# Packet sizes in a DMA-bound rotation: five of twelve slabs loaded with 8 KB and stored with 16 KB packets, the other seven the other way round, and no one-row store first

## The chip, the cores, the metric

One core of one Trainium2 chip; the other cores are idle. The metric is device time in microseconds (us) of one execution, as the median over executions; a profiled execution beside it leaves a trace.

## The reference

```python
x = np.random.randn(32, 3, 256, 256).astype(np.float32)
np.rot90(x, k=-1, axes=(-2, -1)).astype(np.float32)
```

96 images of 256 x 256 float32 are turned by a quarter. Nothing is computed: 25.17 MB come in and 25.17 MB go out.

## The kernel before

The 96 images are cut into 12 slabs of 8 images, 2.10 MB each (called "2 MB" below, and half of it "1 MB"). A slab lies in a tile of 128 partitions x 2 x 2048 float32. What decides the size of a DMA packet is how much of one partition is contiguous in device memory: 8 rows of 1 KB (the `(n i p r)` views, 128 partitions) give 8 KB packets; 16 rows (the `(n i m r)` view, 64 partitions for one half) give 16 KB packets. Half `i` of a 16 KB slab lies in every second partition, `units[n][i::2]`.

```python
    RI, RO = 16, 8
    ...
    plain = (0, last - 2, last - 1, last)
    ...
    ld8_v  = rows_in.rearrange("(n i p r) w -> n p i (r w)", i=I, p=P, r=RO)
    ld16_v = rows_in.rearrange("(n i m r) w -> n i m (r w)", i=I, m=Q * K, r=RI)
    st_v   = rows_out.rearrange("(n i p c) w -> n p i (c w)", i=I, p=P, c=RO)
    ...
    for n in range(n_slabs):              # all loads are issued first, on the sync queue
        for i in range(I):
            if n in plain:
                nc.sync.dma_start(out=units[n][:, i], in_=ld8_v[n][:, i])
            else:
                nc.sync.dma_start(out=units[n][i::I].rearrange("p i f -> p (i f)"), in_=ld16_v[n, i])

    for n in range(n_slabs):              # slab n is turned into the tile of slab n - 1
        t_in, t_out = units[n], units[n - 1] if n else turned0    # slab 0 into PSUM
        ...                               # two VectorE transposes of 128 x 2048 for each slab
        if n == 1:
            nc.sync.dma_start(out=st_v[n][:, 0, :W], in_=t_out[:, 0, :W])      # the one-row store
            nc.sync.dma_start(out=st_v[n][:, 0, W:], in_=t_out[:, 0, W:])
            nc.sync.dma_start(out=st_v[n][:, 1], in_=t_out[:, 1])
        elif n in (2, 3):
            for i in range(I):
                nc.sync.dma_start(out=st_v[n][:, i], in_=t_out[:, i])
        elif n:
            nc.sync.dma_start(out=st_v[n], in_=t_out)

    for i in range(I):                    # slab 0 last: PSUM -> SBUF by ScalarE, then stored
        nc.scalar.copy(out=units[last][:, i], in_=turned0[:, i])
    nc.sync.dma_start(out=st_v[0], in_=units[last])
```

So before, slabs 0, 9, 10 and 11 are loaded and stored in 8 KB packets, slabs 1 to 8 loaded in 16 KB and stored in 8 KB. The first store goes out as one row (1 KB) of each partition, then the other seven.

## Time and profile before

| | before |
|---|---|
| time | 123.53 us (123.49 to 123.58, 3 runs) |
| span of the profiled execution | 121.8 us |
| 16 DMA engines busy | 98.1% of the span |
| VectorE busy | 92.7 us (76%), 24 transposes |
| packets | 5888, of which 640 are semaphore writes |

How to read it: the page cuts the span into 40 slices; the DMA row has the busy share of 16 DMA engines in tenths, the GB/s row what they moved. The prediction below shows these rows.

One more reading of the trace is used throughout the document. For every packet the trace has a start, a duration and a size. Spreading each packet's bytes evenly over its duration and adding up the engines gives the bytes moved up to each moment; the time between two successive multiples of 2.10 MB is the time that the queue needed for one slab.

### The profile page before, as it was taken

To read this page: it belongs to the slowest core of one execution; us is meant where nothing else is said; L and a number is where in the kernel's file an instruction comes from. 1 tells how busy PE (TensorE), PEld (TensorE's weight loads), DVE (VectorE), ACT (ScalarE), POOL (GpSimd) and SP (SyncE) were. 2 spreads that over 40 slices of the span, in tenths; PEclk is the share of its full clock that TensorE was granted. 3 is DMA by queue.
4 is the path that set the end of the run, shared out by engine and by line. 5 is a ranking of instruction groups with operands and counts; after the bars stand their busy time and mean duration, and the time that the engine had idled before them with its cause. 6 is when DMAs were issued, how large, how long until landed. Compare 5 with 4: busy or idle time off the path is not lost.

```text
span 121.8 us, 140 instructions
## 1 busy us (share of the span) xinstructions
DVE 92.7 (76%) x24; ACT 5.0 (4%) x3; POOL 0.2 (0%) x4
## 2 busy tenths in 40 slices
DVE  0199999999999999999999999999999930000000
ACT  0000000000000000000300000000000660000000
POOL 0000000000000000000000000000000000000000
DMA  3999999999999999999999999999999999999995
GB/s 86 425 436 430 430 430 430 430 430 430 430 430 430 430 430 403 430 422 420 420 397 429 430 425 425 430 425 430 428 430 430 428 430 430 425 425 428 425 430 218
DMA packets 5888, 50.33 MB, mean 413 GB/s; under 512 B 640, under 2 KB 768, under 8 KB 896
## 3 DMA queue, kind: packets, MB, share of 16 engines
q1 hardware_dynamic: 5888, 50.33, 98.1%
HBM read 25.17 MB, written 25.17 MB: 413 GB/s over the span
## 4 chain that ended last, share of the span: by engine, by line
DVE 41%; issue 33%; DMA 4%; DVEq 3%; ACT 2%
DVE u L80 31%; DVE turned L74 6%; DMA u<-in_x_dram 4%; DVE u L74 4%; DVEq L120 3%; ACT u L93 2%
## 5 line engine op out<-in xcount | busy, mean ns | idle before, releaser
L80 DVE STREAM_TRANSPOSE u<-u 128x2048 f32<-128x2048 f32 x16 | 62.4, 3945 | 0.3
L74 DVE STREAM_TRANSPOSE u<-u 128x2048 f32<-128x2048 f32 x6 | 22.8, 3931 | 0.0
L74 DVE STREAM_TRANSPOSE turned<-u 128x2048 f32<-128x2048 f32 x2 | 7.6, 3828 | 5.6 <-DMA u<-in_x_dram 5.6
L93 ACT COPY u<-turned 128x2048 f32<-128x2048 f32 x2 | 3.7, 1865 | 35.8 <-DVE u L74 35.8
L93 ACT ACT_TABLE_LOAD x1 | 1.3, 1283 | 59.7 <-DMA u<-in_x_dram 59.7
L109 POOL MEMSET const-bfloat16-1.0<- 128x1 bf16 x1 | 0.1, 101 | 0.0
L109 POOL MEMSET const-uint8-127<- 128x1 uint8 x1 | 0.1, 101 | 0.0
L109 POOL MEMSET const-float32-0.0<- 128x1 f32 x1 | 0.1, 98 | 0.2 <-issue 0.2
L109 POOL MEMSET const-float32-1.0<- 128x1 f32 x1 | 0.1, 98 | 0.0
## 6 DMA issues: line engine op xcount, KB each, us to landing
u<-in_x_dram SPq DMA_DIRECT2D x24, 1024.0 KB, 19.6
out_dram<-u SPq DMA_DIRECT2D x9, 2048.0 KB, 22.8
out_dram<-u SPq DMA_DIRECT2D x5, 1024.0 KB, 17.4
out_dram<-u SPq DMA_DIRECT2D x1, 896.0 KB, 17.5
out_dram<-u SPq DMA_DIRECT2D x1, 128.0 KB, 18.0
```

The costliest lines, as they stand in the source:

```text
L74: nc.vector.transpose(out=dst[:, :, ::-1, ::-1], in_=src)
L80: nc.vector.transpose(out=dst[:, cs], in_=src[:, cs])
L93: nc.scalar.copy(out=units[last][:, i], in_=turned0[:, i])
L109: nc = _bacc.Bacc("TRN2", target_bir_lowering=False, num_devices=1)
L120: with _tile.TileContext(nc) as tc:
```

## The change

Each quarter turn has a row side and a column side, and by choice of the layout in SBUF one of the two can have 16 KB packets. The intent: give every slab one 16 KB side (four had none), choose which side per slab, and drop the one-row store. Slabs 0, 1, 2, 10 and 11 are now loaded in 8 KB and stored in 16 KB packets, slabs 3 to 9 loaded in 16 KB and stored in 8 KB.

```diff
-    plain = (0, last - 2, last - 1, last)
+    long_st = (0, 1, 2, last - 1, last)
 ...
     for n in range(n_slabs):
+        if n in (1, 2, last - 1):
+            ld = nc.sync.dma_start(out=units[n], in_=ld_short[n])
+            continue
         for i in range(I):
-            if n in plain:
-                nc.sync.dma_start(out=units[n][:, i], in_=ld8_v[n][:, i])
+            if n in long_st:
+                ld = nc.sync.dma_start(out=units[n][:, i], in_=ld_short[n][:, i])
             else:
-                nc.sync.dma_start(out=units[n][i::I].rearrange("p i f -> p (i f)"), in_=ld16_v[n, i])
+                ld = nc.sync.dma_start(out=units[n][i::I].rearrange("p i f -> p (i f)"), in_=ld_long[n, i])
+
+    def store(n, t, i):
+        if n in long_st:
+            return nc.sync.dma_start(out=st_long[n, i], in_=t[i::I].rearrange("p i f -> p (i f)"))
+        return nc.sync.dma_start(out=st_short[n][:, i], in_=t[:, i])
 ...
-        if n in plain:
-            for i in range(I):
-                src = t_in[:, i].rearrange("p (r g c) -> p c r g", r=RO, c=RO)
-                dst = t_out[:, i].rearrange("p (c g r) -> p c r g", c=RO, r=RO)
-                nc.vector.transpose(out=dst[:, :, ::-1, ::-1], in_=src)
+        if n in long_st:
+            src = t_in.rearrange("p i (r g c) -> p c r g i", r=RS, c=RL)
+            dst = t_out.rearrange("p i f -> p (i f)").rearrange("p (c k r) -> p c r k", c=RL, r=RS)[:, :, ::-1, ::-1]
+            pieces = 2
+            for h in range(pieces):
+                cs = slice(h * RL // pieces, (h + 1) * RL // pieces)
+                nc.vector.transpose(out=dst[:, cs], in_=src[:, cs])
 ...  (the 16 KB load form keeps its transposes)
-        if n == 1:
-            nc.sync.dma_start(out=st_v[n][:, 0, :W], in_=t_out[:, 0, :W])
-            nc.sync.dma_start(out=st_v[n][:, 0, W:], in_=t_out[:, 0, W:])
-            nc.sync.dma_start(out=st_v[n][:, 1], in_=t_out[:, 1])
-        elif n in (2, 3):
+        if n in range(5, last - 1):
+            nc.sync.dma_start(out=st_short[n], in_=t_out)
+        elif n:
             for i in range(I):
-                nc.sync.dma_start(out=st_v[n][:, i], in_=t_out[:, i])
-        elif n:
-            nc.sync.dma_start(out=st_v[n], in_=t_out)
+                store(n, t_out, i)
 ...
-    nc.sync.dma_start(out=st_v[0], in_=units[last])
+    for i in range(I):
+        store(0, units[last], i)
```

More of the change, by code (lines that the diff above doesn't have):

```diff
@@ L40, with short, long @@
     P = nc.NUM_PARTITIONS
-    RI, RO = 16, 8
-    K = H // RI
+    RL, RS = 16, 8
     I = 2
-    Q = P // (K * I)
+    Q = P * RS // H
     n_slabs = B * C // (Q * I)
     last = n_slabs - 1
-    plain = (0, last - 2, last - 1, last)
-    F = RO * W
+    F = RS * W
+    long_st = (0, 1, 2, last - 1, last)
     rows_in = x.rearrange("b c h w -> (b c h) w")
     rows_out = out.rearrange("b c h w -> (b c h) w")
-    ld8_v = rows_in.rearrange("(n i p r) w -> n p i (r w)", i=I, p=P, r=RO)
-    ld16_v = rows_in.rearrange("(n i m r) w -> n i m (r w)", i=I, m=Q * K, r=RI)
-    st_v = rows_out.rearrange("(n i p c) w -> n p i (c w)", i=I, p=P, c=RO)
+    def short(rows):
+        return rows.rearrange("(n i p r) w -> n p i (r w)", i=I, p=P, r=RS)
+    def long(rows):
+        return rows.rearrange("(n i m r) w -> n i m (r w)", i=I, m=P // I, r=RL)
+    ld_short, ld_long, st_short, st_long = short(rows_in), long(rows_in), short(rows_out), long(rows_out)
     pools = [ctx.enter_context(tc.tile_pool(name=f"unit{u}", bufs=1)) for u in range(n_slabs)]
@@ L68 @@
+    def store(n, t, i):
+        if n in long_st:
+            return nc.sync.dma_start(out=st_long[n, i], in_=t[i::I].rearrange("p i f -> p (i f)"))
+        return nc.sync.dma_start(out=st_short[n][:, i], in_=t[:, i])
     for n in range(n_slabs):
         t_in, t_out = units[n], units[n - 1] if n else turned0
-        if n in plain:
-            for i in range(I):
-                src = t_in[:, i].rearrange("p (r g c) -> p c r g", r=RO, c=RO)
-                dst = t_out[:, i].rearrange("p (c g r) -> p c r g", c=RO, r=RO)
-                nc.vector.transpose(out=dst[:, :, ::-1, ::-1], in_=src)
-        else:
-            src = t_in.rearrange("p i f -> p (i f)").rearrange("p (r g c) -> p c r g", r=RI, c=RO)
-            dst = t_out.rearrange("p i (c k r) -> p c r k i", c=RO, r=RI)[:, :, ::-1, ::-1, :]
-            for h in range(2):
-                cs = slice(h * RO // 2, (h + 1) * RO // 2)
-                nc.vector.transpose(out=dst[:, cs], in_=src[:, cs])
@@ L82 @@
-        if n == 1:
-            nc.sync.dma_start(out=st_v[n][:, 0, :W], in_=t_out[:, 0, :W])
-            nc.sync.dma_start(out=st_v[n][:, 0, W:], in_=t_out[:, 0, W:])
-            nc.sync.dma_start(out=st_v[n][:, 1], in_=t_out[:, 1])
-        elif n in (2, 3):
-            for i in range(I):
-                nc.sync.dma_start(out=st_v[n][:, i], in_=t_out[:, i])
-        elif n:
-            nc.sync.dma_start(out=st_v[n], in_=t_out)
+        if n in long_st:
[5 more added lines that the diff above has]
+                nc.vector.transpose(out=dst[:, cs], in_=src[:, cs])
+        else:
+            src = t_in.rearrange("p i f -> p (i f)").rearrange("p (r g c) -> p c r g", r=RL, c=RS)
+            dst = t_out.rearrange("p i (c k r) -> p c r k i", c=RS, r=RL)[:, :, ::-1, ::-1, :]
+            for h in range(2):
+                cs = slice(h * RS // 2, (h + 1) * RS // 2)
+                nc.vector.transpose(out=dst[:, cs], in_=src[:, cs])
```

## The prediction

> **What bounds the kernel now.** I read the utilisation slices first, then the DMA queue's total, the groups of instructions, stretches of the span, packet counts of two clean stretches, and last the issue order. The slices and the queue come first because a rotation computes nothing: it moves 25.17 MB in, 25.17 MB out.
>
> ```profile
> DVE  0199999999999999999999999999999930000000
> DMA  3999999999999999999999999999999999999995
> GB/s 86 425 436 430 430 430 430 430 430 430 430 430 430 430 430 403 430 422 420 420 397 429 430 425 425 430 425 430 428 430 430 428 430 430 425 425 428 425 430 218
> q1 hardware_dynamic: 5888, 50.33, 98.1%
> ```
>
> The 16 DMA engines are full from the second slice to the last but one. VectorE, which does all transposes, is also dense but ends seven slices earlier. So the transfers set the end. 50.33 MB at 428 GB/s is 117.6 us of the 121.8 us span; the remaining 4.2 us are the start until the first bytes move (first slice, 86 GB/s), a few dips, and the end (last slice, 218 GB/s).
>
> The page's chain of waits names VectorE for 41% of the span. I do not follow it: it passes through program order, its last steps being the transposes at 90.9 us and a ScalarE copy at 98.63 us, and leaves the last 20 us of store traffic unexplained. The groups show what VectorE costs:
>
> ```profile
> L80 DVE STREAM_TRANSPOSE u<-u 128x2048 f32<-128x2048 f32 x16 | 62.4, 3945 | 0.3
> L74 DVE STREAM_TRANSPOSE u<-u 128x2048 f32<-128x2048 f32 x6 | 22.8, 3931 | 0.0
> L74 DVE STREAM_TRANSPOSE turned<-u 128x2048 f32<-128x2048 f32 x2 | 7.6, 3828 | 5.6 <-DMA u<-in_x_dram 5.6
> L93 ACT COPY u<-turned 128x2048 f32<-128x2048 f32 x2 | 3.7, 1865 | 35.8 <-DVE u L74 35.8
> ```
>
> The two forms of transpose, line 80 (16 KB load, 8 KB store) and line 74 (8 KB both ways), cost the same within 0.4%. The only wait is 5.6 us for the first load. The timeline ends with
>
> ```profile
> 98.63 1.86 ACT L93 COPY u<-turned 128x2048 f32<-128x2048 f32 x1 [1.91 <-DVE u L74]
> 100.52 0.37 SPq L94 DMA_DIRECT2D out_dram<-u  x1
> ```
>
> The last store is issued at 100.52 us and its semaphore arrives at about 121.0 us: 20.5 us, of which 4.9 us are its own 2 MB. It waits 15.6 us behind other stores. That is the slack on the compute side.
>
> Now the rate by stretch (last column), and then the packets of two stretches, 10 to 45 us (only 16 KB loads) and 75 to 115 us (only 8 KB stores):
>
> ```profile
> 10.00:45.00 35.00, 34.83 (x10) 0.00 (x0) 0.00 (x0) 1.00 1.01 430
> 47.00:60.00 13.00, 12.97 (x4) 0.28 (x1) 0.00 (x0) 1.00 1.02 423
> 60.00:64.00 4.00, 3.97 (x2) 1.00 (x1) 0.00 (x0) 1.00 1.00 396
> 75.00:115.00 40.00, 23.56 (x7) 3.73 (x2) 0.00 (x0) 1.00 1.01 428
> ```
> ```profile
> DMA packets 1147, 15.04 MB, mean 430 GB/s; under 512 B 229, under 2 KB 229, under 8 KB 229
> ```
> ```profile
> DMA packets 2217, 17.11 MB, mean 428 GB/s; under 512 B 128, under 2 KB 128, under 8 KB 128
> ```
>
> The small packets are semaphore writes. The trace's packet records give 309 ns for 8 KB, 611 for 16 KB and 9 for a semaphore write, each overlapping the next by 3 to 4 ns; so an 8 KB packet takes 305.7 ns of an engine, a 16 KB one 607.5, a semaphore 5.7. Check from the fences: (35 us x 16 - 229 x 0.0057) / 918 = 608.6 ns, and (40 x 16 - 128 x 0.0057) / 2089 = 306.0 ns. So joining two 8 KB packets saves 4 ns of 611: 0.65%. That is all the gain the packet size can give. The 8 KB loads late in the program (47 to 60 us) run at 423, about 1.6% below 16 KB loads; the 396 at 60 to 64 us is the turn from loads to stores with the one-row store in it.
>
> **What the Trainium skill says.** "DMA: Bandwidth & Descriptors", section "Where 436 GB/s comes from", puts the ceiling at 435.2 GB/s. The trace agrees (428 to 430). An estimate from that page: 50.33 MB / 435.2 = 115.7 us, so even perfect transfers would gain about 1.9 us against the 117.6 above: less than 2%. The same page, "Why small descriptors are slow (HBM only)", states a fixed overhead of about 3 cycles per packet; with that page's 850 MHz, 3.5 ns as an estimate, close to the 4 ns above. Its "Why a DMA increments its semaphore by 16 and not by 1" says the engine count is the largest number up to 16 that divides the slowest dimension, so 64 rows still use 16 engines; the 16 KB loads (64 partitions each) confirm it with 430 GB/s. "SBUF — State Buffer", section "Door 1: The DMA port swizzle", warns that partitions 0 to 63 reach only half of the ports. The 64 partitions here are every second one of 128, which reach all ports; the loads show no loss, but no store in this form has run yet.
>
> **The change, part by part.** Per engine, from the durations above; 1 MB is 8 packets of 8 KB or 4 of 16 KB. A 2 MB slab of 8 KB stores in one DMA: 16 x 305.7 + 5.7 = 4897 ns. As 16 KB stores in two DMAs: 2 x (4 x 607.5 + 5.7) = 4871 ns.
> - Stores of slabs 0, 10, 11: -26 ns each, -78.
> - Store of slab 2 (two DMAs before, 4903): -32.
> - Store of slab 1: before 8 x 42.4 (1 KB) + 8 x 268.3 (7 KB) + 8 x 305.7 + 3 x 5.7 = 4948; after 4871: -77.
> - Store of slab 4: split into two DMAs, +6. Slab 3 unchanged, 5 to 9 unchanged.
> - Loads of slabs 1 and 2: 16 KB becomes 8 KB, one DMA each: about +16 each, +32.
> - Load of slab 9: 8 KB becomes 16 KB in the stretch where 8 KB loads run at 423 and not 430: 2.10 MB / 423 - 2.10 MB / 430 = -80. Load of slab 10 in one DMA: -6.
> Sum: -78 - 32 - 77 + 6 + 32 - 80 - 6 = -235 ns, on the path, since the engines are never idle.
>
> VectorE: still 24 transposes of 128x2048, at 3.83 to 3.95 us by the rows above, so about 92.7 us. But a slab's first transpose now needs both 1 MB halves of its load, where a plain slab's needed one. VectorE starts 2.45 us later (1 MB / 428 GB/s): at 8.05 us instead of 5.6, and ends at about 101.0 instead of 98.6. Both ScalarE copies now wait for the last transpose (before, the first ran at 94.9, during it): 101.0 + 2 x 1.87 = 104.8 us with hand-over. The queue reaches slab 11's store at 121.0 - 2 x 4.9 = 111.2 and slab 0's at 116.1. Slack stays 10.2 and 11.3 us; none of it shows in the time. Issues on the sync queue stay 40 (24 + 16 before, 21 + 19 after).
>
> **The rivals.**
> 1. The turn to stores costs more without the small first store. The 396 GB/s stretch lost 4 x (1 - 396/428) = 0.30 us; a few load packets there took 470 to 580 instead of 309 ns. If the one-row store was softening this, 16 KB first packets could double the loss: -0.235 + 0.3 = +0.07 us, 123.6. If it was itself the trouble, the loss could halve: 123.15. The profile cannot tell which.
> 2. Stores from every second partition read SBUF worse than loads write it. Against: the same pattern as a load is at full rate. If it halved the rate, five slabs would take 4.9 us more each: +24 us, about 148. I give this 2 to 3%.
> 3. VectorE becomes the bound. The new transpose form (8 KB load, 16 KB store) covers 10 of 24 instructions; it must take 10.2 / 10 = 1.0 us more each before the stores run dry. The two known forms differ by 14 ns. Every further 0.1 us on each would add 1 us to the end; about 1%.
> 4. The whole effect is larger, because 16 KB stores gain more than the record of 16 KB loads says. Loads at 430 already carry excess of 1 to 3 ns; stores had none. At the ceiling of 435.2 the five slabs gain 10.49 MB x (1/428 - 1/435.2) = 0.41 us: 123.0.
>
> **Range and chances.** 123.53 - 0.235 = 123.3 us. Rivals 1 and 4 span 123.0 to 123.6, so 122.95 to 123.7 should hold 8 times in 10. Faster by over 2% needs 2.5 us, more than the distance to the ceiling: 1%. Slower by over 2% is rivals 2 and 3: 3%. The rest, 96%, is within 2%.
>
> **What would show it.** Right: the same 9s in the DMA row to the last slice; 5248 packets in all (before 5888 less 640 semaphore writes = 5248 data packets; 512 fewer by joining, 128 fewer without the cut rows: 4608; again 40 issues x 16 = 640 semaphore writes); 429 to 430 GB/s where slabs 10, 11 and 0 are stored; VectorE starting near 8 us and ending near 101; last issue near 105; span near 121.5. Wrong: gaps or a lower rate in the store slices of slabs 1, 2, 10, 11, 0 (rival 2), a new transpose row well over 3.95 us (rival 3), or a deeper dip than 397 at the turn (rival 1).

## The result, and the profile after

| | before | after |
|---|---|---|
| median, first set of rounds | 123.60 us (6 runs) | 123.44 us (6 runs) |
| median, second set of rounds | 123.82 us (11 runs) | 123.58 us (6 runs) |
| ratio after / before, first set | | 0.9981 (95%: 0.9964 to 0.9998) |
| ratio after / before, second set | | 0.9984 (95%: 0.9968 to 0.9999) |

A ratio is the mean time of one kernel's fast runs over that of the other's of the same rounds, so not quite the ratio of the medians. The change gains about 0.2 us, 0.16 to 0.19%; the two sets agree, and both 95% intervals just exclude no change.

The slices, the packet counts and the queue's total of the changed kernel:

```profile
DVE  0039999999999999999999999999999993000000
DMA  3999999999999999999999999999999999999994
GB/s 83 425 425 431 428 447 431 431 431 431 431 431 420 425 431 420 401 428 423 420 434 431 431 417 428 423 423 431 431 431 425 431 431 428 455 431 431 431 431 178
DMA packets 5248, 50.33 MB, mean 414 GB/s; under 512 B 640, under 2 KB 640, under 8 KB 640
q1 hardware_dynamic: 5248, 50.33, 97.9%
```

The DMA row is as full as before. 5248 packets are the number that the prediction counted. Each GB/s value credits a packet to the slice where it starts, so single slices swing: the four 431 near the end are the 16 KB stores of slabs 10, 11 and 0, where before had 425 to 430, but some slices of 8 KB stores also show 431. The slab times below tell the two apart. VectorE starts one slice later.

The groups (busy us, mean ns of one, then the idle time before them and its end):

```profile
L95 DVE STREAM_TRANSPOSE u<-u 128x2048 f32<-128x2048 f32 x14 | 54.7, 3956 | 0.2
L89 DVE STREAM_TRANSPOSE u<-u 128x2048 f32<-128x2048 f32 x8 | 31.3, 3986 | 0.1
L89 DVE STREAM_TRANSPOSE turned<-u 128x2048 f32<-128x2048 f32 x2 | 7.1, 3586 | 8.2 <-DMA u<-in_x_dram 8.2
L104 ACT COPY u<-turned 128x2048 f32<-128x2048 f32 x2 | 3.6, 1868 | 40.5 <-DVE u L89 40.5
```

The new transpose form (line 89) takes 3.99 us against 3.96 for the other: VectorE did not become a bound. The wait for the first load is 8.2 us instead of 5.6. The end of the timeline:

```profile
93.73 13.41 SPq L78 DMA_DIRECT2D out_dram<-u  x6
101.58 3.63 ACT L104 COPY u<-turned 128x2048 f32<-128x2048 f32 x2 [40.51 <-DVE u L89]
```

Both copies run after the last transpose, from 101.58 to 105.2 us; the last stores are issued there, 10 us and more before the queue gets to them.

The same stretches as in the prediction (us, busy times, then DMA share and GB/s); 10 to 17 us is now an 8 KB load, 47 to 60 us mixes slab 9 in 16 KB with slabs 10 and 11 in 8 KB:

```profile
10.00:45.00 35.00, 34.86 (x10) 0.00 (x0) 0.00 (x0) 1.00 1.01 430
47.00:60.00 13.00, 12.96 (x4) 0.21 (x1) 0.00 (x0) 1.00 1.00 419
60.00:64.00 4.00, 3.97 (x2) 1.07 (x1) 0.00 (x0) 1.00 1.03 432
75.00:115.00 40.00, 26.44 (x7) 3.63 (x2) 0.00 (x0) 1.00 1.02 431
```

The row that moved most is the turn from loads to stores, 60 to 64 us: 432 GB/s, before 396. Packets of 16 KB that start at the edge of so short a stretch count whole (47 to 60 us even reads lower than before, 419 against 423, although slab 9 got faster), so the size of the gain is taken from the slab times. There are two traces of each kernel:

| part of the queue's work | before (two traces) | after (two traces) | change | predicted |
|---|---|---|---|---|
| slab 0 is in, from the span's start | 7.51, 7.56 | 7.52, 7.53 | -0.01 | 0 |
| load of slab 1 | 4.883, 4.869 | 4.900, 4.904 | +0.026 | +0.016 |
| load of slab 2 | 4.868, 4.868 | 4.939, 4.917 | +0.060 | +0.016 |
| loads of slabs 3 to 8 | 29.30, 29.33 | 29.37, 29.37 | +0.053 | 0 |
| load of slab 9 | 4.965, 4.963 | 4.897, 4.896 | -0.068 | -0.080 |
| load of slab 10 | 4.973, 4.972 | 4.966, 4.966 | -0.007 | -0.006 |
| load of slab 11 and store of slab 1 (the turn) | 10.078, 10.067 | 9.885, 9.951 | -0.155 | -0.077 |
| store of slab 2 | 4.906, 4.906 | 4.871, 4.871 | -0.035 | -0.032 |
| stores of slabs 3, 5 to 9 | 29.41, 29.41 | 29.40, 29.40 | 0.00 | 0 |
| store of slab 4 | 4.900, 4.900 | 4.906, 4.906 | +0.006 | +0.006 |
| stores of slabs 10 and 11 | 9.800, 9.800 | 9.737, 9.737 | -0.063 | -0.052 |
| store of slab 0 and the rest, to the span's end | 6.25, 6.47 | 6.29, 6.29 | -0.07 | -0.026 |
| span | 121.84, 122.11 | 121.69, 121.73 | -0.265 | -0.235 |

The two spans of the kernel before are 0.27 us apart, as much as the change of the mean, so the rows are worth more than the last line.

A slab of 16 KB stores takes 4.869 us, one of 8 KB stores 4.900 (in one transfer) or 4.906 (in two), in every trace. The loads are dearer than predicted and the turn cheaper; the experiments look into both.

### The profile page after: what moved, and what is told of

Its sections match the earlier page's. It is cut to its first block, busy times and chain, and to the rows that moved or that the text cites. A ratio compares the mean times of both kernels' runs of the same rounds, so it can differ in the third digit from the quotient of the medians.

```text
span 121.7 us, 138 instructions
## 1 busy us (share of the span) xinstructions
DVE 93.0 (76%) x24; ACT 4.9 (4%) x3; POOL 0.2 (0%) x4
## 2 busy tenths in 40 slices
DMA packets 5248, 50.33 MB, mean 414 GB/s; under 512 B 640, under 2 KB 640, under 8 KB 640
## 3 DMA queue, kind: packets, MB, share of 16 engines
q1 hardware_dynamic: 5248, 50.33, 97.9%
## 4 chain that ended last, share of the span: by engine, by line
DMA 60%; DVE 13%; issue 7%; DVEq 3%; ACT 2%; ACTq 1%; SPq 0%
DMA u<-in_x_dram 42%; DMA out_dram<-u 18%; DVE u L89 7%; DVE u L95 7%; DVEq L132 3%; ACT u L104 2%; ACTq L132 1%; SPq L72 0%; SPq L79 0%
## 5 line engine op out<-in xcount | busy, mean ns | idle before, releaser
L89 DVE STREAM_TRANSPOSE turned<-u 128x2048 f32<-128x2048 f32 x2 | 7.1, 3586 | 8.2 <-DMA u<-in_x_dram 8.2
```

Of the source, the lines that this page charges most:

```text
L89: nc.vector.transpose(out=dst[:, cs], in_=src[:, cs])
```

## The experiments

Twelve kernels ran, in three sets; those of one set shared a chip and the runs of the kernel before (medians 123.72, 123.61 and 123.82 us). Single executions of the kernel before lay between 123.43 and 124.14 us, so the trace decides where hundredths matter.

**1. before_again: the kernel before, unchanged.**

> The kernel before, unchanged, to learn how far the packet records repeat. From the first trace, the time that the queue needed for one 2 MB slab: 4.87 us for the loads of slabs 1 to 3, 4.89 for slab 8, 4.97 for slabs 9 and 10, 5.13 for slab 11 (the turn to stores), 4.95 for the store of slab 1, 4.90 for the later stores. If these repeat within 0.01 us, differences of 0.02 to 0.07 us per slab between kernels mean something; if they scatter by 0.05 us, they do not, and only timed rounds count.

One run: 123.9 us, span 122.11. Slabs 1 to 3 took 4.87 us, slab 8 4.90, slabs 9 and 10 4.96 and 4.97, slab 11 5.12, the first store 4.94, later stores 4.90: each within 0.02 us of the first trace. The 0.27 us between the two spans are in the start (0.05) and in the last slab (0.22). Each transfer's semaphore is raised 16 times (640 writes for 40 transfers), once by each engine; the distance from the first to the last of the 16 is how far the engines are apart. In the first trace it was 0.36 us during the loads, 0.47 to 0.59 after the turn and 0.49 at the last transfer; in the second 0.42, then 0.79 to 0.85, and 0.83 at the end. In these two traces an offset taken on at the start or at the turn is still there at the end, and the span ends with the last engine; that is where the two differ. It is no rule: in no_row (below) the distance fell at the turn, from 0.55 to 0.37, and in all_store16 it grew all through the stores, from 0.43 to 0.78.

**2. no_row: the kernel before without the one-row store.**

```diff
-        if n == 1:
-            ...  (row, other seven rows, second half)
-        elif n in (2, 3):
+        if n in (1, 2, 3):
```

> The kernel before without the one-row store: slab 1 stored as two 1 MB halves of 8 KB packets, nothing else. In the changed kernel the last load (slab 11) and the first store (slab 1) took 9.885 us together, before 10.078. Theory A, the one-row store itself makes the turn from loads to stores dear: the two fall to about 9.91 to 9.95 us (the cut rows alone are 0.04 us), total -0.13 to -0.17 us. Theory B, the 16 KB first packets of the changed kernel make the turn cheap: the two stay at about 10.03 (only the cut rows saved), total -0.04 us. Theory C, the one-row store softened the turn: above 10.10 us, total slower.

123.52 us, ratio 0.9988 (0.9976 to 1.0). Last load and first store fell from 10.078 and 10.067 to 9.963 us. Of these 0.11 us, 0.04 are the cut rows: the first half of the store of slab 1 took 2.497 us before and 2.455 here. The other 0.07 are in the last half of the load of slab 11 (2.642 and 2.639 before, 2.569 here). This spoke for theory A; runs 8 and 9 weaken it.

**3. ends_only: the kernel before with only the stores of slabs 10, 11 and 0 in 16 KB packets.**

```diff
+    long_st = (0, last - 1, last)
+    st16_v = rows_out.rearrange("(n i m r) w -> n i m (r w)", i=I, m=Q * K, r=RI)
 ...
+        if n in long_st:            # two transposes in the new form, as in the change
 ...
+        elif n in long_st and n:
+            for i in range(I):
+                nc.sync.dma_start(out=st16_v[n, i], in_=t_out[i::I].rearrange("p i f -> p (i f)"))
 ...
-    nc.sync.dma_start(out=st_v[0], in_=units[last])
+    for i in range(I):
+        nc.sync.dma_start(out=st16_v[0, i], in_=units[last][i::I].rearrange("p i f -> p (i f)"))
```

> The kernel before with only the stores of slabs 10, 11 and 0 in 16 KB packets (their loads were 8 KB already). The theory of 4 ns per joined packet: 4.87 us instead of 4.90 us for the stores of slabs 10 and 11, about 0.02 to 0.03 us less for slab 0, so -0.08 us in all, with loads, the turn and the other stores unchanged. The rival, that stores from every second partition read worse: any of the three above 4.90 us. In time about -0.06%, which five rounds may not resolve; the packet records decide.

The stores of slabs 10 and 11 took 4.870 and 4.868 us, as the 4 ns theory says, and the loads of slabs 1 to 10 were as before; last load and first store, the same transfers as before, took 10.036 us. Yet the time was 123.81 us, ratio 1.0014 (1.0002 to 1.0026), no gain but a small loss. What grew in the trace is the closing: from the last packet's end to the span's end 1.32 us, where before had 1.15 in both traces; that is more than the 0.06 us saved on the two stores. What the sync queue waited for at the end, here and in the changed kernel (total us, times, longest):

```profile
SPq L133 <- DMA out_dram<-u: 14.2, 1, 14.2
```
```profile
SPq L132 <- DMA out_dram<-u: 13.6, 5, 4.0
```

The transfers use eight semaphores in turn, and the program ends with a row of waits on all of them in a fixed order, 0.06 us apart. This kernel has 43 transfers, so the semaphore of the last one is tested early: one long wait of 14.2 us, and the others still have to be gone through after it. With 40 transfers, before and after, the last transfer's semaphore is in the last of these waits, and the earlier ones have been passed while stores were still running. Over all 14 traces: 40 transfers closed in 1.14 to 1.19 us, 39 in 1.22, 38, 41 and 42 in 1.27 to 1.29, 43 in 1.31 and 1.32, 45 in 1.50. What counts is not the number itself but how many of these waits stand behind the last transfer's. From the last semaphore to the span's end it took 0.79 to 0.83 us with none behind (40 transfers), 0.85 to 0.88 with one (39, 41), 0.92 to 0.94 with two (38, 42), 0.97 to 1.01 with three (43, 45). The rest of the 1.50 is a last semaphore that came 0.49 us after the last packet, not 0.32 to 0.37 as in most traces. The change kept 40.

**4. no_compute: the changed kernel's transfers without transposes and copies (wrong result).**

```diff
     for n in range(n_slabs):
-        t_in, t_out = units[n], units[n - 1] if n else turned0
-        ...  (transposes)
+        t_out = units[n]
 ...
-    for i in range(I):
-        nc.scalar.copy(out=units[last][:, i], in_=turned0[:, i])
     for i in range(I):
-        store(0, units[last], i)
+        store(0, units[0], i)
```

> The changed kernel's transfers alone, with no transpose and no copy (a wrong result on purpose): same loads, same stores, same order. In the changed kernel the queue took 4.94 us for the load of slab 2, 4.90 us for slabs 3 to 9 and 4.97 us for slab 10, where 4.90 us (8 KB packets) and 4.87 us (16 KB) are what the quiet stretches show. Theory D, VectorE writing SBUF disturbs loads: without it 16 KB loads take 4.87 us and 8 KB loads 4.90 us throughout. Theory E, the loads slow down by themselves (more transfers queued, or the engines drifting against each other): 4.89 to 4.90 and 4.94 to 4.97 us remain. The turn and the stores should not change: 4.87 us for 16 KB stores, 4.90 us for 8 KB.

Theory E. 123.41 us in its one run, as fast as the changed kernel with its work. Stretches of this kernel (no engine works but the DMA), and of the changed kernel:

```profile
18.00:47.00 29.00, 0.00 (x0) 1.00 1.01 428
53.00:60.00 7.00, 0.00 (x0) 1.00 1.01 422
```
```profile
18.00:47.00 29.00, 28.86 (x9) 0.00 (x0) 0.00 (x0) 1.00 1.01 429
53.00:60.00 7.00, 6.96 (x3) 0.21 (x1) 0.00 (x0) 1.00 1.02 424
```

The load of slab 2 took 4.924 us (4.939 with the work), slabs 3 to 9 4.892 to 4.899, slab 10 4.965: VectorE has no part in the slow loads. The Trainium skill says the same in "SBUF — State Buffer", section "SBUF: two separate sides": DMA and engine accesses use separate ports. This run agrees.

**5 to 7. Which slabs have the 16 KB side.** In the changed kernel only the tuple of slabs with 16 KB stores differs (and which loads or stores go as one transfer):

```diff
-    long_st = (0, 1, 2, last - 1, last)
+    long_st = ()                          # all_load16: 16 KB loads, 8 KB stores
+    long_st = (0, 1)                      # two_long
+    long_st = tuple(range(n_slabs))       # all_store16: 8 KB loads, 16 KB stores
```

> The changed kernel with every slab loaded in 16 KB and stored in 8 KB packets. Two open points. First, where loads begin to slow down: theory F, after about 40 packets per engine (so it looks in both kernels: the kernel before after 16 + 3 x 8, the changed one after 16 + 16 + 8): here 40 packets of 16 KB are 5 slabs, so slabs 1 to 4 load in 4.87 us and slabs 5 to 11 in 4.89. Theory G, after a time or an amount (5 to 8 MB, 14 to 22 us): slabs 3 and 4 already show 4.88 to 4.89. Second, the total: late 8 KB loads cost 4.97 us where 16 KB loads cost 4.89 (0.075 more), 16 KB stores save only 0.03 against 8 KB ones; so against the kernel before the loads of slabs 9 to 11 give -0.22 us, the missing row about -0.11: ratio about 0.9973. If 16 KB stores mattered more than that, it would be no faster than the changed kernel, 0.998.

> The changed kernel with only slabs 0 and 1 loaded in 8 KB and stored in 16 KB packets, all others loaded in 16 KB and stored in 8 KB. By the measured prices per slab: against the changed kernel, slab 2 loads in 4.87 instead of 4.94 us, slabs 3 and 4 about 0.01 to 0.03 less, slabs 10 and 11 0.07 less each; the stores of 2, 10 and 11 0.03 more each: about -0.14 us, so ratio to the kernel before about 0.997. By theory F the slow loads start at slab 3 (16 + 16 + 8 packets), by G between slabs 2 and 4. The rival is that 16 KB loads just before the turn, or 8 KB stores at the end, give the gain back: then 0.998 or above.

> The changed kernel the other way: every slab loaded in 8 KB and stored in 16 KB packets. Theory F: 40 packets are 2.5 slabs, so slabs 0 and 1 load at 4.90, slab 2 at 4.94, slabs 3 to 11 at 4.97 us. Theory G: the same onset between 5 and 8 MB (slab 2 to 4), so here the two differ little. All 12 stores take 4.87 us. Against the changed kernel: loads of slabs 3 to 9 +0.07 each = +0.5 us, stores of 3 to 9 -0.03 each = -0.22: +0.28 us, ratio to the kernel before about 1.000.

| | time, ratio (95%) | slabs 1 to 4 | slab 5, 6 | slabs 7 to 10 | last load and first store |
|---|---|---|---|---|---|
| all_load16 | 124.26, 1.0051 (1.0038 to 1.0065) | 4.868 each | 4.871, 4.882 | 4.892 to 4.896 | 10.173 |
| two_long | 123.74, 1.001 (0.9998 to 1.0023) | 4.907, 4.872, 4.882, 4.892 | 4.894, 4.894 | 4.894 to 4.897 | 10.061 |
| all_store16 | 124.14, 1.0039 (1.0026 to 1.0053) | 4.903, 4.916, 4.969, 4.968 | 4.971, 4.968 | 4.968 to 4.971 | 9.846 |

Where the loads slow down: theory F. With 16 KB loads throughout, slabs 3 and 4 are still at 4.868 us, after 8 MB and 22 us, where the kernel before was already rising, and the rise comes in slabs 5 and 6. With 8 KB loads throughout it comes in the second half of slab 2. In all 14 traces it sets in between about 40 and 48 packets per engine, and not at a time or an amount (15 to 17 us in the changed kernel, 27 to 32 us in all_load16), nor at a number of transfers (within the 4th and within the 11th or 12th). What happens there is open. Its price is shown: 16 KB loads rise from 4.868 to 4.894 us per slab, 8 KB loads from 4.90 to 4.97; per packet that is much alike, 3.3 ns (8 packets per engine and slab) and 4.4 ns (16). The 8 KB loads of all_store16 by stretch:

```profile
8.00:15.00 7.00, 6.84 (x2) 0.00 (x0) 0.00 (x0) 1.00 1.01 428
20.00:58.00 38.00, 37.83 (x10) 0.00 (x0) 0.00 (x0) 1.00 1.01 421
```

My prices per slab held (stores 4.869 against 4.900, late loads 4.97 against 4.89), but the sums did not: all_load16 should have been 0.27% faster than before and was 0.51% slower. Its profiled span is 0.67 us longer than the changed kernel's mean of 121.71: the start +0.28 (first bytes at 2.05 us instead of 1.75), the loads of slabs 1 to 10 -0.26, the turn +0.26, the stores of slabs 2 to 11 +0.11, and +0.28 in the last slab and the closing (engines 0.7 us apart at the end instead of 0.5, and 43 transfers instead of 40). two_long missed likewise (expected 0.997): a turn of 10.061 us, and 42 transfers with a closing of 1.27. all_store16 came out 0.4% above what I expected, 45 transfers closing in 1.50 us and engines 0.78 us apart at the end, while its turn was the cheapest of all. Each of these accounts rests on one trace.

**8. after_row: the changed kernel with a one-row store put back.**

```diff
-        elif n:
+        elif n == 1:
+            row = t_out[0::I].rearrange("p i f -> p (i f)")
+            nc.sync.dma_start(out=st_long[1, 0][:, :W], in_=row[:, :W])
+            nc.sync.dma_start(out=st_long[1, 0][:, W:], in_=row[:, W:])
+            store(1, t_out, 1)
+        elif n:
```

> The changed kernel with the one-row store put back: of the first 16 KB store, the first 1 KB row of 64 partitions goes ahead, then the remaining 15 KB. If the row is what makes the turn dear (as its removal from the kernel before showed, 10.08 to 9.96 us for the last load and the first store together), these two go from 9.885 to 9.95 to 10.0 us here, of which the 64 extra cut rows are 0.02; time +0.05 to +0.1 us against the changed kernel. If the turn is cheap here because the first store packets are 16 KB, it stays below 9.91.

123.47 us, ratio 0.9988 (0.9976 to 1.0001). Last load and first store took 9.892 us: the cut rows show (2.459 instead of 2.441 us for the first half of the store), but the last load did not get slower (4.998; 5.009 and 5.078 without the row). So the row did not make the turn dear in this trace.

**9. after_again: the changed kernel once more.**

> The changed kernel, unchanged, for more timed rounds beside the next three and for a second trace. From the first trace: first bytes at 1.76 us, slab 0 loaded at 7.52, loads of slabs 1 to 10 together 49.07, last load and first store 9.885, stores of slabs 2 to 11 48.92. Ratio to the kernel before again 0.997 to 0.999. If last load and first store repeat only within 0.05 us, the part of the one-row store in them is smaller than the scatter.

Ratio 0.9984. Everything repeated within 0.02 us but the turn: 9.951 us against 9.885, a scatter of 0.07. That is as much as the part of no_row's gain that is not cut rows. So of the turn's -0.155 us, 0.073 are the rows no longer cut and the 16 KB packets of the store of slab 1 (4.947 to 4.875 us, rounded means of the two traces of each); the other 0.08, in the load of slab 11, are seen in both traces but not explained. Three more traces lie on the same two sides: slab 11 took 5.091 us in ends_only (loads and first store of the kernel before), 5.043 in no_compute and 4.998 in after_row (loads of the changed kernel).

**10 to 12. Three more choices of slabs**, to test what the first runs suggested, that the first and the last load must be in 8 KB packets:

```diff
-    long_st = (0, 1, 2, last - 1, last)
+    long_st = (0, 1, last)                # three_long; stores of slabs 2 to 10 in one transfer each
+    long_st = (0, 1, 2, last - 1)         # last16
+    long_st = (1, 2, last - 1, last)      # first16
```

> A candidate for the best: 8 KB loads and 16 KB stores only for slabs 0 (first to load), 1 and 11 (last to load); all others 16 KB loads and 8 KB stores. The theory from the runs so far: the first load must be 8 KB (with 16 KB it came 0.28 us later), the last load before the turn must be 8 KB (with 16 KB last load and first store took 10.06 to 10.17 us, with 8 KB 9.85 to 9.96), everything else is best loaded in 16 KB. Against the changed kernel: loads of slabs 2 -0.07, 3 -0.02, 10 -0.07; stores of 2 +0.03, 10 +0.03, 3 and 4 in one transfer -0.01: -0.11 us, ratio to the kernel before about 0.9972; last load and first store 9.88 to 9.92. The rival, that more than one slab of 8 KB loads is needed before the turn: last load and first store above 10.0, ratio 0.998 to 1.000.

> The changed kernel with one slab turned over: slab 11, the last to be loaded, is loaded in 16 KB and stored in 8 KB packets. If the packet size of the last load sets the cost of the turn, last load and first store take 10.03 to 10.10 us instead of 9.885, though 16 KB loads are otherwise quicker; the store of slab 11 4.906 instead of 4.868: +0.2 us, ratio to the kernel before about 1.000. The rival, that first-store size or chance made the turns of the earlier runs differ: they take 9.81 to 9.88 us, ratio 0.998.

> The changed kernel with slab 0, the first to be loaded, loaded in 16 KB and stored in 8 KB packets. If the size of the first packets sets the start, first bytes are recorded at 2.05 us and not 1.76, and slab 0 is in at 7.80 us and not 7.52; its store 0.03 more: +0.3 us, ratio to the kernel before about 1.0005. The rival, that the late start of the all-16 KB kernel was chance: slab 0 in at 7.45 to 7.55 us, ratio 0.998.

three_long was meant to be the best and was 124.11 us, ratio 1.0019 (1.0001 to 1.0037). Loads and stores cost what was expected (loads of slabs 1 to 10 48.90 us, 0.16 less than the changed kernel's 49.06), but last load and first store took 10.384 us although the last load is in 8 KB packets. Its rate by slices, with 340 at the turn:

```profile
GB/s 110 415 426 450 442 428 428 428 428 428 428 428 428 428 428 428 428 428 399 340 461 402 428 426 428 428 428 428 426 428 428 428 428 428 428 428 461 428 428 129
```

last16 was 123.60 us, ratio 0.9983 (0.9966 to 0.9999), as fast as the changed kernel, with last load and first store at 9.915 us although the last load is in 16 KB packets. Both went against my theory of the turn, so it falls: the size of the last load's packets does not by itself set its cost.

first16 was 123.87 us, ratio 1.0012 (0.9992 to 1.0031). The part on the start was right: first bytes at 2.09 us, slab 0 in at 7.85. Its last load and first store, the same transfers as the changed kernel's, took 10.126 us, 0.2 more; its six runs lay between 123.74 and 124.25 us and the profiled one at 124.2. So the turn is not fixed by the packets on both sides of it. The first two issues of this kernel and of the changed one (start us, us):

```profile
0.73 1.22 SPq L74 DMA_DIRECT2D u<-in_x_dram  x2
```
```profile
0.72 0.88 SPq L72 DMA_DIRECT2D u<-in_x_dram  x2
```

A first transfer of 64 rows in 16 KB packets is issued more slowly and its first packet starts 0.3 us later. With all_load16 (2.05, 7.80) two kernels show it, and the twelve other traces with an 8 KB first load begin at 1.74 to 1.77 us.

The packet records show where a dear turn loses its time: in the last 3 us of the loads some packets take up to double. Counted are those over 60 ns longer than the usual 309 or 611 ns: none in all_store16 (turn 9.846), 3 in the changed kernel (9.885), 12 in the kernel before (10.078), 28 in first16 (10.126), 40 in three_long (10.384; 373 to 716 ns). The order is not strict (4 in before_again, 10.067). Why these packets wait was not tested.

## Why the prediction was right

- **The bound.** Right. The DMA row is full to the end in both kernels, and taking all compute away (no_compute) left 123.41 us.
- **16 KB stores from every second partition** read at full rate: rival 2 is refuted by 4.869 us per slab. The store terms were right to 0.014 us in total (-0.035, +0.006, -0.063 against -0.032, +0.006, -0.052); ends_only shows them alone.
- **Slabs 9 and 10.** Right: -0.068 and -0.007 us.
- **Loads of slabs 1 to 8: the mis-sized term.** The step took +16 ns each for slabs 1 and 2 and nothing for 3 to 8; it measured +0.026, +0.060 and +0.053 us, +0.14 in all instead of +0.03. A slip is in it: by the prediction's own durations one 8 KB transfer against two of 16 KB is 4897 against 4871 ns, +26 and not +16, and +0.026 is what slab 1 measured. Beyond that I had taken the quiet early packets for all of slab 2. The slow-down after 40 to 48 packets per engine, which 8 KB loads reach earlier, is what the step did not know; all_load16 and all_store16 show it.
- **The turn.** I left it at its cut rows and packets, -0.077, with rival 1 either way. It measured -0.155: the direction of rival 1's friendly branch, but not its reason, for with the row put back (after_row) the turn stayed cheap. The rival's size of 0.30 us was read from one 4 us stretch; by the slab times the turn before cost 0.16 us more than its packets (10.078 against 9.92). What makes a turn cheap is not settled: neither the row (after_row), nor the last load's size (last16, three_long), nor both neighbours' sizes (first16), nor compute (no_compute, 9.921) decides it, and over all kernels it lay between 9.85 and 10.38 us.
- **The sum.** +0.12 us on the loads against -0.08 at the turn and -0.04 in the last slab nearly cancel, so the total (-0.235 predicted, -0.265 by the spans, about -0.2 by the timed rounds) owes part of its accuracy to luck. Of the -0.265 about half is shown by packets and cut rows (-0.13 with the predicted -0.026 for slab 0); the rest, in the load of slab 11 and in the start and end of the program, is measured but not explained.
- **VectorE's slack.** Right: it ends at 101.5 us (predicted 101.0) and the last issue comes at 105.8 (104.8). Rival 3 needed 1.0 us more per transpose; the new form took 0.03 more. The transposes into PSUM even got quicker, 3.59 us instead of 3.83.
- **Rival 4**, larger packets gaining more on stores than on loads: hardly. 4.869 against 4.906 us, both in two transfers, is 4.6 ns for each of the 8 pairs joined per engine, where the prediction had 4.0.

No kernel tried beat the changed one clearly; last16 equals it.

## What to carry to other kernels

When the DMA queue is full from end to end, price every packet size per direction from the trace before choosing: here 16 KB instead of 8 KB packets save 0.03 us per 2 MB stored, 0.07 us per 2 MB loaded late and 0.03 early, while the first transfer should have small packets (0.3 us). At this level the fixed parts weigh as much as the packets: the turn from loads to stores, how far the engines are apart at the end, and even the number of transfers, which decides how many closing waits come after the last one. Add up the parts before believing a better total: three_long and all_load16, both better than the changed kernel by their prices per slab, came out slower than even the kernel before; in the one trace of each, the turn, the end and for all_load16 the start took more than the packets saved. What makes a turn dear is not known, so such a sum is tested and not trusted.

## What the Trainium skill lacked or had wrong

- "DMA: Bandwidth & Descriptors", section "Why small descriptors are slow (HBM only)", has a fixed cost per packet that is near that of stores (4.6 ns measured per packet saved; 3.5 ns is an estimate from the page's 3 cycles and 850 MHz), but nothing on loads slowing down after 40 to 48 packets per engine: 4.90 to 4.97 us per 2 MB in 8 KB packets, 4.868 to 4.894 in 16 KB.
- The same page, section "Latency and other measured facts", gives about 600 ns to the first byte for transfers issued from the sync queue. It does not say from where it counts. Here the first packet starts 1.03 us after its issue begins (0.725 to 1.754 us) and 0.64 us after it ends with 8 KB packets, which agrees if counted from the end; with 16 KB packets it is 1.36 and 0.78 us (first16).
- No page gives the size of the engines' spread: 0.3 to 0.6 us among the 16 through the loads, changed mostly at the turn, and 0.35 to 1.0 us at the end, where the last one sets the time.
- No page has the cost of the turn from loads to stores: the last load and first store together took 9.85 to 10.38 us, where their packets at the prices of late loads and of stores would take 9.76 to 9.92; the excess went from 0.01 (all_store16) to 0.55 us (three_long).
- "SBUF — State Buffer", section "Door 1: The DMA port swizzle", has no case of every second partition: 64 of them load and store at 4.868 us per 2 MB, 431 GB/s.
- No page says that closing waits over the DMA semaphores can lie behind the last transfer: from the last semaphore to the end 0.79 to 0.83 us with 40 transfers, 0.97 to 1.01 with 43 and 45.
